# A hybrid decoder layer on one core: five pairs of split weight tiles and four loaded ones instead of four and three

## The chip, the core and the metric

The kernel runs on one core of a Trainium2 chip. A core has five engines with their own instruction queues: TensorE (PE) multiplies matrices, VectorE (DVE), ScalarE (ACT) and GpSimd (POOL) work on elements, SyncE (SP) issues transfers. The metric is the device time of one execution in microseconds; three executions of the kernel before gave 1117.61 to 1118.88 us, median 1118.25 us.

## The reference

One layer of a decoder is computed for 1024 prompt tokens and 8 x 4 sample tokens (T = 1056 tokens of width 1024), in 32-bit floating point:

```
h = rms(x) ;  z = h @ w_in               -> q (512) | k (128) | v (128) | u (512)
a = sliding-window attention(q, k, v)       128 keys, 8 heads, 2 key heads, learned sinks
m = (trailing mean of u, windows 2/4/8/16, minus u) @ w_pool * pool_scale
x = x + rms([a | m] @ w_out)
f = rms(x) ;  f = (silu(f @ w_gate) * (f @ w_up)) @ w_down      width 2816
x = x + rms(f)
x = x + sigmoid(x @ w_ple_gate) * (p @ w_ple)
```

The results are x for both kinds of tokens and the updated key, value and pooling buffers.

## The kernel before

**Products.** Each 32-bit operand is split into a high part in PE's fast format and the low remainder, and a product is made of three: high x high, high x low and low x high (`gemm`, L278). `split` (L163) makes the two parts: ACT casts the high one (L164) and DVE subtracts it to get the low one (L165). The tokens are taken in three groups of 352 columns (g = 0, 1, 2), so almost all matmuls are 128 x 128 by 128 x 352.

**Weights.** Every weight tile of 128 x 1024 numbers (4 KB on each partition) comes through two rings. SP loads it into a raw tile (tag `wr`, W_RAW tiles; `w_load`, L169), and `w_split` (L180) splits it into a pair of tiles (tag `wp`, 2 * W_PAIRS tiles). A ring's tile is given out again when its last user is done: a raw tile when the split has read it, a pair when PE has done its last matmul with it. `weights(j)` (L191) splits up to W_PAIRS - 1 tiles ahead and loads one more; it serves the projections with its default, and the output projections with a count given in the call. `need(k)` (L264) does the same in the FFN and the last stage, four items ahead (LOOK = 4), whatever W_PAIRS is.

```python
def w_load(j):
    ...
    t = wpool.tile(shape, F32, tag="wr", bufs=W_RAW, name=nm("wr"))
    nc.sync.dma_start(t, src)
    ...
def w_tile(shape, s):
    return wpool.tile(shape, F32R, tag="wp", bufs=2 * W_PAIRS, name=nm(s))
    ...
def weights(j, ahead=W_PAIRS - 1):
    for i in range(j, j + (0 if lazy[0] else ahead) + 1):
        w_split(i)
        w_load(i + 1)
```

**Start.** x and the four column tiles of u are loaded in halves in an order pinned on SP (`load`, L342); three of the u tiles use the `wr` ring, the fourth another pool. ACT and DVE make the x operands (L366, L368) and, for the norm, the squares and their sum `acc` (L377, L331 to L334). w_pool (`wpl`, L424) also takes a `wr` tile, then the projections' weights do.

**Attention.** Projections of k, v, q, then blocks of 128 queries, with parts of the output projection as filler between them. The order on PE is that of the program from the u products on.

**FFN.** The hidden width is taken in 11 slabs of two column tiles. Five slabs are first computed for group 2 alone, then six for all three groups, then the first five again for groups 0 and 1 (`WALK`). Groups 0 and 1 are taken together with one product less: POOL makes four sums of the quarters of a gate and an up tile in place (`w_sums`, L990), and ACT and DVE split them into two pairs (`sh`, `sl`). So a column tile takes a pair for gate (jg), one for up (ju) and two for the sums, and a slab two for its part of w_down. The down products of a slab (`down`) run after the gate products of the next slab's first column tile; their results go from PSUM into `o` by DVE (L1087). `hid` is the operand of the down products, made by `hid_put` from `u` (L1068) and `c` (L1061). PE's results stand in eight PSUM banks, each free again when DVE or ACT has read it.

**Last stage.** While groups 0 and 1 go through their last slabs, group 2 is normed (L1115, L1119; `ple_steps`), and then the same happens to groups 0 and 1 beside the final products (`ple_out`).

**The order of the work.** PE's order is pinned. On DVE, ACT, POOL and SP a planner that comes with the language writes the order before the run: it replays the program with its own durations, takes at each engine the earliest instruction of the program that is ready and for which a tile is free, and puts in the waits. Only instructions marked with `keep_in_program_order` keep their place behind the one before. On the chip each queue is worked off strictly in the written order.

Of the kernel before, what the change touches and what calls it, by code (L numbers as in the profile page):

```python
# [47 lines left out]
UEXT = PST + DSEQ  # L48
ULEN = UPRE + SEQ + NDEC * UEXT

W_PAIRS = 4
W_RAW = 3


WARM = 8
# [6 lines left out]
def trunk_kernel(  # L62
# [43 lines left out]
    def nm(s):  # L106
        cnt[0] += 1
        return f"{s}{cnt[0]}"

    def act_tile(shape, dt=F32, s="a"):  # L110
        return apool.tile(shape, dt, tag="a", bufs=A_SLOTS, name=nm(s))
# [57 lines left out]
    def w_load(j):  # L169
        if j >= len(plan) or j in raws:  # L170
            return
        src, shape = plan[j]
        t = wpool.tile(shape, F32, tag="wr", bufs=W_RAW, name=nm("wr"))
        nc.sync.dma_start(t, src)
        raws[j] = t

    def w_tile(shape, s):
        return wpool.tile(shape, F32R, tag="wp", bufs=2 * W_PAIRS, name=nm(s))

# [10 lines left out]
# [5 lines that stand above are left out]
        return pairs[j]  # L195
# [145 lines left out]
    def load(dst, src):  # L341
        tc.keep_in_program_order(nc.sync.dma_start(dst, src))  # L342
# [38 lines left out]
    def u_load(c, h):  # L381
        j = U0[c]
        if h == 0:
            shape = plan[j][1]
            raws[j] = act_tile(shape) if c == 3 else wpool.tile(shape, F32, tag="wr", bufs=W_RAW, name=nm("wr"))
        load(raws[j][:, 4 * h : 4 * h + 4, :], plan[j][0][:, 4 * h : 4 * h + 4, :])
# [34 lines left out]
    for dst, src in ((psc, pscale), (skp, sink_p), (skd, sink_d)):  # L421
        load(dst, src)
    wpl = wpool.tile([P, 4, P], F32, tag="wr", bufs=W_RAW, name="wpl")
    nc.sync.dma_start(wpl, w_pool)  # L424
# [852 lines left out]
```

## Time and profile before

| what | value |
|---|---|
| profiled execution | 1118.37 us, its span 1116.6 us |
| median of three executions | 1118.25 us |
| PE busy | 1106.5 us (99%), 7171 matmuls |
| DVE busy | 748.3 us (67%) |
| ACT busy | 440.0 us (39%) |
| POOL busy | 179.4 us (16%) |
| granted PE clock, mean | 0.998 |
| DMA | 99.54 MB, mean 89 GB/s |

The span is the time from the first to the last instruction. In a list of waits, a row gives who waited, what released it, and the total, the count and the longest in us. In a timeline, a row gives start and length in us, the engine, the line, the operation with out<-in, shapes and count, and in brackets the idle time of the engine before it and what ended it; PEld are the weight loads of PE. In a table of windows, a row gives the window and its length, the busy time of PE, PEld, DVE, ACT and POOL with the number of instructions, PE's granted clock, the DMA share and GB/s. Matmuls overlap: the profile draws each about 0.32 us long although the next starts 0.16 us later.

### The profile page before, as it was taken

How to read it: one execution, taken by the hardware profiler on the slowest of the kernel's cores; microseconds unless marked ns; L12 is line 12 of the kernel's file. 1: busy time of each engine (PE TensorE's matmuls, PEld its weight loads, DVE VectorE, ACT ScalarE, POOL GpSimd, SP SyncE). 2: the span in 40 equal slices, each digit the busy share in tenths (PEclk: the TensorE clock that was granted, in tenths of full speed). 3: DMA queues.
4: the chain of work that ended last, by engine and by line, in shares of the span. 5: the costliest groups of instructions: out<-in, count | busy, mean ns of one | idle time of the engine just before them, and what ended most of it. 6: DMA issues, size and time to landing. Idle time of an engine off the chain costs nothing.

```text
span 1116.6 us, 17703 instructions
## 1 busy us (share of the span) xinstructions
PE 1106.5 (99%) x7171; PEld 1089.6 (98%) x7171; DVE 748.3 (67%) x1241; ACT 440.0 (39%) x779; POOL 179.4 (16%) x152
## 2 busy tenths in 40 slices
PE   8999999999999999999999999999999999999998
PEld 8999988899999999999999999999999999999998
DVE  6667478886979955255564555547887877789532
ACT  8323276664645523331222313123424334365220
POOL 0045032200000131011111102112132123100000
PEclk9999999999999999999999999999999999999999
DMA  8121311542543212121120202122112222336211
GB/s 289 56 71 38 122 43 38 194 157 85 203 166 129 99 38 76 39 76 39 38 60 17 78 36 76 38 100 79 57 58 83 70 76 80 124 133 222 85 58 39
DMA packets 35217, 99.54 MB, mean 89 GB/s; under 512 B 4132, under 2 KB 14660, under 8 KB 35136
## 3 DMA queue, kind: packets, MB, share of 16 engines
q1 hardware_dynamic: 33808, 96.65, 25.5%
q10 hardware_dynamic: 1328, 1.77, 0.5%
q8 instruction: 56, 0.92, 0.3%
q14 instruction: 25, 0.20, 0.1%
HBM read 88.30 MB, written 10.11 MB: 88 GB/s over the span
## 4 chain that ended last, share of the span: by engine, by line
PE 93%; DVE 3%; DMA 1%; issue 1%; POOL 1%; ACT 1%; SPq 0%; DVEq 0%; POOLq 0%
PE b L126 92%; PE b L120 1%; DMA xr<-in_x_dram 1%; DVE wl L165 1%; POOL wr L990 0%; SPq L342 0%; DVE h L368 0%; DVE o L1115 0%; DVE x L1119 0%; DVE mx L628 0%; DVE a L736 0%; DVE p L1024 0%; DVE hid L165 0%; ACT h L366 0%; ACT xr L377 0%
## 5 line engine op out<-in xcount | busy, mean ns | idle before, releaser
L126 PE MATMUL b<-fh,wh 128*128 128x352 f32 x808 | 260.7, 323 | 0.0
L126 PE MATMUL b<-fh,wl 128*128 128x352 f32 x808 | 259.3, 321 | 0.0
L126 PE MATMUL b<-fl,wh 128*128 128x352 f32 x808 | 259.0, 321 | 0.0
L126 PE MATMUL b<-hid,wh 128*128 128x352 f32 x1056 | 252.5, 322 | 1.8 <-DVE o L1115 1.2
L164 ACT CAST wh<-wr 128x1024 fp32r<-128x1024 f32 (+1 forms) x139 | 143.0, 1031 | 248.9 <-PE b L126 205.6
L165 DVE TENSOR_TENSOR wl<-wr,wh 128x1024 fp32r<-128x1024 f32 (+1 forms) x139 | 170.5, 1229 | 57.9 <-ACT wh L164 53.9
L126 PEld LDWEIGHTS b<-hid,wh 128*128 128x128 f32 x1056 | 182.3, 188 | 2.6 <-issue 1.5
L126 PE MATMUL b<-hid,wl 128*128 128x352 f32 x528 | 169.0, 320 | 0.0
L990 POOL TENSOR_TENSOR wr<-wr 128x512 f32<-128x512 f32 x44 | 63.4, 1441 | 623.0 <-DVE wl L165 621.3
L126 PEld LDWEIGHTS b<-fl,wh 128*128 128x128 f32 x808 | 151.9, 188 | 0.0
L126 PEld LDWEIGHTS b<-fh,wl 128*128 128x128 f32 x808 | 151.8, 188 | 0.0
L126 PEld LDWEIGHTS b<-fh,wh 128*128 128x128 f32 x808 | 151.6, 188 | 0.0
L1087 DVE TENSOR_TENSOR o<-o,b 128x352 f32<-128x352 f32 x240 | 114.9, 516 | 29.3 <-PE b L126 29.3
L126 PE MATMUL b<-fh,sh 128*128 128x352 f32 x352 | 113.6, 323 | 0.0
L126 PE MATMUL b<-fl,sh 128*128 128x352 f32 x352 | 112.7, 320 | 0.0
L126 PE MATMUL b<-fh,sl 128*128 128x352 f32 x352 | 112.7, 320 | 0.0
L126 PE MATMUL b<-h,wh 128*128 128x352 f32 x480 | 105.5, 325 | 0.9 <-ACT h L366 0.6
L165 DVE TENSOR_TENSOR sl<-wr,sh 128x1024 fp32r<-128x1024 f32 x44 | 53.8, 1222 | 75.5 <-ACT sh L164 75.5
L126 PEld LDWEIGHTS b<-hid,wl 128*128 128x128 f32 x528 | 98.9, 187 | 0.0
L164 ACT CAST sh<-wr 128x1024 fp32r<-128x1024 f32 x44 | 45.7, 1047 | 130.9 <-POOL wr L990 91.2
L126 PEld LDWEIGHTS b<-h,wh 128*128 128x128 f32 x480 | 81.9, 189 | 2.2 <-DVE h L368 1.2
L126 PE MATMUL b<-h,wl 128*128 128x352 f32 x240 | 66.3, 326 | 0.0
(150 smaller groups left out, 1591.0 us busy)
## 6 DMA issues: line engine op xcount, KB each, us to landing
wr<-in_w_gu_dram SPq DMA_DIRECT2D x64, 512.0 KB, 3.3
wr<-in_w_dn_dram SPq DMA_DIRECT2D x32, 512.0 KB, 3.3
wr<-in_w_pg_dram SPq DMA_DIRECT2D x14, 512.0 KB, 3.6
x<-in_x_dram SPq DMA_DIRECT2D x6, 704.0 KB, 7.1
x1d<-x SPq DMA_DIRECT2D x6, 704.0 KB, 3.5
x<-x1d SPq DMA_DIRECT2D x6, 704.0 KB, 6.7
out_y_dram<-yo SPq DMA_DIRECT2D x24, 176.0 KB, 1.9
wr<-in_w_out_b_dram SPq DMA_DIRECT2D x8, 512.0 KB, 3.3
```

The source lines that it names most:

```text
L120: ins = te.transpose(out, src, ident)
L126: ins = te.matmul(*args, **kw)
L164: fix(se.copy(hi, src))
L165: fix(ve.tensor_tensor(lo, src, hi.bitcast(F32), op=ALU.subtract))
L990: ge.tensor_tensor(out, a, b, op=op)
L1087: ve.tensor_tensor(o, o, v, op=ALU.add)
```

## The change

W_PAIRS goes from 4 to 5 and W_RAW from 3 to 4: ten tiles instead of eight in the ring of split weights, four instead of three in the ring of loaded ones, 12 KB more on each partition. The room comes from the scratch space for descriptors of dynamic DMAs, which the toolkit reserves with 16,384 bytes on each partition and which is set to 1,024. `weights` splits four tiles ahead by default instead of three; the counts given in calls and LOOK stay. The sequence of instructions in the program is otherwise the same.

```diff
-W_PAIRS = 4
-W_RAW = 3
+W_PAIRS = 5
+W_RAW = 4
...
-    nc = _bacc.Bacc("TRN2", target_bir_lowering=False, num_devices=1)
+    nc = _bacc.Bacc("TRN2", target_bir_lowering=False, num_devices=1, dynamic_dma_scratch_size=1024)
```

## The prediction

> **What bounds the kernel now.** I read the page first, then what PE waited for, then PE's share by stage.
>
> ```profile
> span 1116.6 us, 17703 instructions
> ...
> PE 1106.5 (99%) x7171; PEld 1089.6 (98%) x7171; DVE 748.3 (67%) x1241; ACT 440.0 (39%) x779; POOL 179.4 (16%) x152
> ...
> PE b L126 92%; PE b L120 1%; DMA xr<-in_x_dram 1%; DVE wl L165 1%; POOL wr L990 0%; SPq L342 0%; DVE h L368 0%; DVE o L1115 0%; DVE x L1119 0%; DVE mx L628 0%; DVE a L736 0%; DVE p L1024 0%; DVE hid L165 0%; ACT h L366 0%; ACT xr L377 0%
> ```
>
> PE is busy 99% of the span and carries the chain that ended last. A change that leaves the 7171 matmuls alone can only win back PE's waits. These are all that PE had late in the run, and the longest at the start:
>
> ```profile
> PE b L126 <- DVE acc L334: 1.3, 1, 1.3
> PE b L126 <- DVE o L1115: 1.2, 1, 1.2
> ...
> PE b L126 <- DVE hid L165: 0.6, 1, 0.6
> PE b L126 <- DVE dg L312: 0.6, 2, 0.4
> ```
>
> By stage (attention's end and first slabs, the middle slabs, the last five slabs, one undisturbed stretch):
>
> ```profile
> 224.00:395.00 171.00, 171.00 (x1097) 170.87 (x1097) 139.30 (x194) 92.53 (x127) 8.13 (x4) 1.00 0.40 137
> 395.00:800.00 405.00, 405.00 (x2554) 405.00 (x2553) 229.47 (x380) 118.97 (x181) 69.85 (x53) 1.00 0.17 56
> 800.00:1000.00 200.00, 197.86 (x1245) 196.84 (x1243) 159.64 (x254) 79.12 (x110) 44.47 (x32) 1.00 0.27 90
> 868.00:896.00 28.00, 28.00 (x179) 28.00 (x177) 23.84 (x38) 10.81 (x14) 5.49 (x4) 1.00 0.23 76
> ```
>
> PE has no gap between 224 and 800; what there is to win lies in the last slabs and at the start. The undisturbed stretch issues 178 matmuls in 28 us, one per 0.157 us, while each is drawn 0.32 us long. So a stall costs its idle time plus about 0.16 us: 1.2 + 0.16 = 1.38 us for L1115, 0.57 + 0.16 = 0.73 for hid.
>
> **The change part by part.** No instruction is added or removed: the 139 pair splits and 44 sum splits, their loads and matmuls stay. Two kinds of room grow, and with them the order that the planner writes for DVE, ACT and SP can move.
>
> *The scratch space.* I cost it at nothing: every data transfer goes through the two hardware queues.
>
> ```profile
> q1 hardware_dynamic: 33808, 96.65, 25.5%
> q10 hardware_dynamic: 1328, 1.77, 0.5%
> ```
>
> *The fifth pair in the last slabs: the stall before 865.* Here is the chain, from PE's sums (fh,sh), gate (fh,wh) and down products (hid) through ACT, DVE and POOL:
>
> ```profile
> 843.85 0.32 PE L126 MATMUL b<-fh,sh 128*128 128x352 f32 x1
> ...
> 851.48 0.32 PE L126 MATMUL b<-fh,wh 128*128 128x352 f32 x1
> ...
> 855.29 0.48 PE L126 MATMUL b<-hid,wh 128*128 128x352 f32 x2
> ...
> 851.51 1.99 ACT L164 CAST wh<-wr 128x1024 fp32r<-128x1024 f32 x2
> ...
> 854.16 1.22 DVE L165 TENSOR_TENSOR wl<-wr,wh 128x1024 fp32r<-128x1024 f32 x1
> ...
> 855.51 1.45 POOL L990 TENSOR_TENSOR wr<-wr 128x512 f32<-128x512 f32 x1 [16.67 <-DVE wl L165]
> ...
> 859.95 1.28 POOL L990 TENSOR_TENSOR wr<-wr 128x512 f32<-128x512 f32 x1
> ...
> 861.27 1.05 ACT L164 CAST sh<-wr 128x1024 fp32r<-128x1024 f32 x1 [2.90 <-POOL wr L990]
> ...
> 856.37 0.98 DVE L165 TENSOR_TENSOR hid<-u,hid 128x352 fp32r<-128x352 f32 x1 [0.55 <-ACT hid L164]
> ...
> 862.35 1.23 DVE L165 TENSOR_TENSOR sl<-wr,sh 128x1024 fp32r<-128x1024 f32 x1 [3.71 <-ACT sh L164]
> 863.50 1.61 DVE L1115 TENSOR_TENSOR o<-o,b 128x1408 f32<-128x1408 f32 x1
> ```
>
> DVE stands still 3.71 us in front of sl while the down products' banks (o L1087, queued behind it) fill up. Then comes L1115, and only then do banks come free: PE ran dry at 865.25 - 1.38 = 863.9. The sums are late because both casts at 851.51 waited until PE finished the sum products at 851.48; the second feeds POOL. With a fifth pair that second cast needs only the sum pair that is done after 36 of the 48 products, 843.85 + 36 x 0.157 = 849.5. The cast takes 1.05 us and the low half 1.22, done at about 851.9. POOL's four steps take 861.23 - 855.51 = 5.7, to 857.6, the cast 1.05, to 858.7. So sl would end near 859.9 instead of 863.6, L1115 at 861.5, before 863.9: the stall goes, -1.38 us. If the order behind sl changes and the cover of free banks is gone, the 1.38 stays; that is the upper end. I take the whole, since the margin is 2.4 us.
>
> *The same room one slab earlier: the stall before 817.5.*
>
> ```profile
> 809.68 1.22 DVE L165 TENSOR_TENSOR wl<-wr,wh 128x1024 fp32r<-128x1024 f32 x1
> 810.82 1.61 DVE L1115 TENSOR_TENSOR o<-o,b 128x1408 f32<-128x1408 f32 x1
> ...
> 812.79 3.15 DVE L1119 SCALAR_TENSOR_TENSOR x<-o,c,x 128x352 f32<-128x352 f32 x2
> 815.85 1.60 DVE L165 TENSOR_TENSOR hid<-u,hid 128x352 fp32r<-128x352 f32 x1
> ...
> 811.03 1.30 POOL L990 TENSOR_TENSOR wr<-wr 128x512 f32<-128x512 f32 x1 [16.49 <-DVE wl L165]
> ...
> 865.46 1.07 DVE L1119 SCALAR_TENSOR_TENSOR x<-o,c,x 128x352 f32<-128x352 f32 x2
> ```
>
> PE wanted hid at 817.51 - 0.73 = 816.8 and got it at 817.45. One low-half split (1.14 us from start to next start) stands ahead of it that a fifth pair lets go earlier; without it hid ends at 816.3. Term -0.73 us, late next nothing on PE. Bounds: 0 if another split takes its place.
> The rows show something else: L1119 costs 1.6 us each while POOL sums run and 0.53 without, hid 1.60 against the 0.98 above. [...] By the rows alone POOL and DVE move together by that split, so I keep -0.73.
>
> *The fourth loaded tile.* In the slabs SP's loads wait for a free tile, not for bandwidth (busy share 0.27 above):
>
> ```profile
> SPq L174 <- DVE sl L165: 446.2, 44, 28.6
> SPq L174 <- DVE wl L165: 413.8, 81, 22.9
> ```
>
> They come one tile earlier; it is what lets the fifth pair be filled in time, and is worth nothing alone as long as the raw has landed before the pair is free. At the start it changes SP's order:
>
> ```profile
> 13.99 0.34 SPq L424 DMA_DIRECT2D wpl<-in_w_pool_dram  x1
> 14.59 3.22 SPq L174 DMA_DIRECT2D wr<-in_w_in_dram  x2
> 17.86 0.43 SPq L342 DMA_DIRECT2D xr<-in_x_dram  x1
> ```
>
> wpl waits for the first weight's tile now and would not then; one more 512 KB load goes ahead of the last x load at 17.86. The page's bandwidth by slices of 27.9 us starts at 289 GB/s:
>
> ```profile
> GB/s 289 56 71 38 122 43 38 194 157 85 203 166 129 99 38 76 39 76 39 38 60 17 78 36 76 38 100 79 57 58 83 70 76 80 124 133 222 85 58 39
> ```
>
> At that rate 256 KB are 0.9 us and 512 KB 1.8 us. The last x load feeds the third group's products, which follow the 192 of the first two groups, 30 us of PE at 0.157 each, so 1.8 us are covered. wpl costs 0.9 us only if it gets ahead of the x loads that PE waits for; they are pinned in order and stand earlier in the program, so 0, with 0.9 as the other end.
>
> *One split more ahead in the projections (the default of weights()).* ACT and DVE do one split (1.05 and 1.22 us) of w_out before attention instead of in it. None of PE's waits listed above lies there. Term 0; if it delayed an eviction that PE needs, at most those 1.22 us.
>
> *The wait before 1000* is the norm of the PLE input behind a split in DVE's queue:
>
> ```profile
> 997.25 1.22 DVE L165 TENSOR_TENSOR wl<-wr,wh 128x1024 fp32r<-128x1024 f32 x1
> ...
> 1000.03 0.43 PE L126 MATMUL b<-dg,c 88*128 88x352 f32 x1 [0.39 <-DVE dg L312]
> ```
>
> It costs 0.39 + 0.16 = 0.55 us and would go if that split moved forward; it could as well be replaced by the next one. I take 0.
>
> Sum: -1.38 - 0.73 = -2.1 us against the profiled execution's 1118.37 us (span 1116.6 and 1.8 around it, 0.1 above the median of the three): 1116.3 us.
>
> **The rivals.** *A deeper cut:* the split before 1000 moves too (-0.55) and the start's wait of 1.3 + 0.16 us for acc is halved (-0.75): 1115.0. For it: DVE's queue is what PE waits for in all of them. Against: nothing in the change touches acc.
> *No gain:* the planner fills the new room and still puts sl where DVE must wait: 1118.4. DVE's own list speaks for it:
>
> ```profile
> DVE sl L165 <- ACT sh L164: 75.5, 27, 6.1
> ```
>
> It waits for sh in slabs without any stall as well, 27 times, and an order that is off by as much is to be had with five pairs too. Against it: those waits lie where PE has more banks in hand.
>
> *Slower:* sl, ready earlier in the planner's reckoning, is put ahead of the last hid in DVE's queue. There it would wait for POOL until 858.7, end at 859.9, and hid would follow at about 860.9. PE needs that hid after the first group's 24 down products (four tiles of six), 855.29 + 24 x 0.157 = 859.1: 1.8 us of stall in each of five slabs, 9.0 us, less the 2.1 won: 1125.3. It decides as soon as sl stands before hid; two slabs of it cancel the gain, and three make it slower by over 0.2% of the time before if only one stall goes. For it: the gap of 0.55 us before hid at 856.37 is just where a planner that counts POOL as quick would place sl. Against: hid is due sooner once the splits before it are gone.
> *A later start:* wpl ahead of the x loads, 0.9 us, and the longer wait brings a second stretch at the lower clock.
>
> ```profile
> 25.00:30.00 5.00, 4.82 (x22) 4.31 (x20) 4.97 (x12) 4.13 (x8) 0.86 (x2) 0.66 0.02 5
> ```
>
> The granted clock was 0.66 in these five us, a loss of 1.7; a second one makes 2.6 in all, and 1118.9 with the late gains.
>
> **How the numbers follow.** Chances: the forecast 0.38, the deeper cut 0.18, no gain 0.12, sl ahead of hid (in some or all slabs) 0.26, the later start 0.06. A measurement of this kernel tells about 0.2% from no change, 2.2 us: faster is below 1116.0, slower above 1120.5. The forecast's own range is 1115.4 to 1117.4, so some 0.12 of its 0.38 falls below 1116.0. Faster 0.18 + 0.12 = 0.30; slower 0.26; the same 0.44. The range from 1114.8 to 1124.0 leaves out half of the deepest cuts and the slower case's last slabs, 0.2 in all.
>
> **What would show it.** Right: PE's waits for L1115 and for hid are gone from the list, POOL's sums in the last slabs start 3 to 4 us earlier against the first down product, and the share of PE in 800 to 1000 is full. Wrong: a wait of PE for hid of one to two us in several slabs, with sl just ahead of it on DVE; PE waits in the attention stage, where now there are none; a wait of PE for acc above 1.3 us; or unchanged starts of POOL's sums, which would say that the pairs were not what held them.

## The result: half a percent slower

The changed kernel takes 1123.08 us (median of 6 runs, 1122.81 to 1123.63), the kernel before beside it 1117.55 us (6 runs, 1116.94 to 1118.88): ratio 1.0049, 95% interval 1.0036 to 1.0062. That is 5.5 us lost where 2.1 us were to be won. The profiled execution took 1122.84 us.

The page of the changed kernel, its span, engines and chain:

```profile
span 1121.0 us, 17674 instructions
...
PE 1107.4 (99%) x7171; PEld 1090.8 (97%) x7171; DVE 758.5 (68%) x1241; ACT 441.6 (39%) x779; POOL 180.9 (16%) x152
...
PE b L126 76%; POOL wr L990 4%; DMA wr<-in_w_gu_dram 2%; PE b L120 1%; DVE sl L165 1%; DMA xr<-in_x_dram 1%; ACT sh L164 0%; SPq L342 0%; DVE h L368 0%; DVE u L1024 0%; DVE mx L628 0%; DVE a L736 0%; ACT h L366 0%; ACT xr L377 0%; POOL a L642 0%
```

The work is the same: 7171 matmuls and nearly as much time on each engine (DVE 758.5 us after 748.3). In the chain POOL's sums (L990) have grown from 0 to 4%, and their low halves (sl) stand in it with 1%. What PE waited for now, largest first:

```profile
PE b L126 <- DVE c L1024: 3.2, 1, 3.2
PE b L126 <- DVE o L1087: 2.1, 2, 1.7
PE b L126 <- DVE dg L312: 1.3, 2, 0.9
...
PE b L126 <- DVE hid L165: 0.9, 1, 0.9
```

The wait for L1115 is gone, as forecast. In its place stand waits of 3.2 us (L1024), 1.7 and 0.4 us (the two for L1087), and the one for hid has grown from 0.6 to 0.9. By stage:

```profile
224.00:395.00 171.00, 171.00 (x1099) 170.98 (x1098) 142.79 (x194) 93.54 (x129) 9.18 (x4) 1.00 0.39 135
395.00:800.00 405.00, 405.00 (x2553) 405.00 (x2553) 240.29 (x380) 121.42 (x180) 70.74 (x52) 1.00 0.17 57
800.00:1000.00 200.00, 193.82 (x1203) 192.26 (x1202) 151.88 (x242) 73.17 (x105) 43.01 (x32) 0.99 0.27 89
```

From 224 to 800 us PE is as full as before; from 800 to 1000 it issues 1203 matmuls instead of 1245. So the loss lies in the last slabs. The slab with the largest wait, DVE first, then the cast of the up tile and its low half, POOL's first sum, the casts of the sums, and the down products on PE with their first row and the row after the wait:

```profile
856.06 0.98 DVE L165 TENSOR_TENSOR hid<-u,hid 128x352 fp32r<-128x352 f32 x1 [0.55 <-ACT hid L164]
860.67 2.36 DVE L165 TENSOR_TENSOR sl<-wr,sh 128x1024 fp32r<-128x1024 f32 x2 [3.63 <-ACT sh L164]
862.95 0.51 DVE L1024 TENSOR_TENSOR c<-p,b 128x352 f32<-128x352 f32 x1
863.38 0.94 DVE L1087 TENSOR_TENSOR o<-o,b 128x352 f32<-128x352 f32 x2
...
848.81 1.05 ACT L164 CAST wh<-wr 128x1024 fp32r<-128x1024 f32 x1 [0.89 <-ACT wh L164]
...
852.32 1.22 DVE L165 TENSOR_TENSOR wl<-wr,wh 128x1024 fp32r<-128x1024 f32 x1
...
853.61 1.51 POOL L990 TENSOR_TENSOR wr<-wr 128x512 f32<-128x512 f32 x1 [18.05 <-DVE wl L165]
...
859.59 1.99 ACT L164 CAST sh<-wr 128x1024 fp32r<-128x1024 f32 x2 [3.56 <-POOL wr L990]
...
854.44 0.32 PE L126 MATMUL b<-hid,wh 128*128 128x352 f32 x1
...
863.51 0.66 PE L126 MATMUL b<-hid,wh 128*128 128x352 f32 x1 [3.19 <-DVE c L1024]
```

Both low halves of the sums now stand directly behind hid in DVE's queue, ahead of c and of every down result o. DVE waits 3.63 us for POOL and ACT, then works 2.3 us on the two, and reads no bank from 857.0 to 862.95. PE has started the down products at 854.44 and runs out of banks at 863.51 - 3.35 = 860.2 (the 3.19 in brackets and the 0.16 that the prediction adds to each wait). Before, two results were read first, and the second low half came five results later. Its cast had waited for PE, which was still using the pair of tiles that it needed. The kernel before, DVE and then ACT:

```profile
857.71 0.94 DVE L1087 TENSOR_TENSOR o<-o,b 128x352 f32<-128x352 f32 x2
862.35 1.23 DVE L165 TENSOR_TENSOR sl<-wr,sh 128x1024 fp32r<-128x1024 f32 x1 [3.71 <-ACT sh L164]
...
865.03 0.51 DVE L1087 TENSOR_TENSOR o<-o,b 128x352 f32<-128x352 f32 x1
...
866.45 1.81 DVE L1087 TENSOR_TENSOR o<-o,b 128x352 f32<-128x352 f32 x4
868.17 1.22 DVE L165 TENSOR_TENSOR sl<-wr,sh 128x1024 fp32r<-128x1024 f32 x1
...
863.01 1.05 ACT L164 CAST sh<-wr 128x1024 fp32r<-128x1024 f32 x1 [0.69 <-PE b L126]
```

In the changed kernel a stretch at half the clock follows the wait:

```profile
857.00:860.00 3.00, 3.00 (x20) 3.00 (x20) 0.04 (x1) 0.41 (x1) 2.48 (x2) 1.00 0.00 0
860.00:863.40 3.40, 0.33 (x3) 0.04 (x1) 2.73 (x4) 1.58 (x2) 0.00 (x0) 1.00 0.14 31
863.50:866.90 3.40, 3.39 (x12) 3.39 (x13) 3.40 (x6) 0.50 (x1) 0.00 (x0) 0.50 0.78 270
```

In the 3.4 us after it the granted clock is 0.50, and PE issues 12 matmuls, which at 0.159 us each would take 1.9 us: 1.5 us lost. In the window ahead, from 860.0 to 863.4 us, PE worked 0.33 us. Behind the waits of 1.71 us (ended at 910.89) and 0.88 us (at 816.50) the clock stays at 1.00 in the same trace. I take the long wait for the cause; what sets the clock is not shown.

The sum for this pair of traces: late waits of 3.35, 1.87, 0.4 + 0.16 and 0.88 + 0.16 us for L1024, L1087 twice and hid, 6.8 in all, and 1.5 for the clock, against 2.1 before: 6.2 us. The spans differ by 4.4, and the changed kernel's profiled execution was some 1.4 us ahead by the end of attention, so that 5.8 us were lost behind it. The starts differ from trace to trace: of these two, only the kernel before has a stretch at clock 0.50 near 25 us. So I make nothing of that part.

### The profile page after: what moved, and what is told of

Its sections match the earlier page's. It is cut to its first block, busy times and chain, and to the rows that moved or that the text cites. A ratio compares the mean times of both kernels' runs of the same rounds, so it can differ in the third digit from the quotient of the medians.

```text
span 1121.0 us, 17674 instructions
## 1 busy us (share of the span) xinstructions
PE 1107.4 (99%) x7171; PEld 1090.8 (97%) x7171; DVE 758.5 (68%) x1241; ACT 441.6 (39%) x779; POOL 180.9 (16%) x152
## 4 chain that ended last, share of the span: by engine, by line
PE 77%; issue 12%; POOL 5%; DVE 3%; DMA 2%; ACT 1%; SPq 0%; POOLq 0%; DVEq 0%
PE b L126 76%; POOL wr L990 4%; DMA wr<-in_w_gu_dram 2%; PE b L120 1%; DVE sl L165 1%; DMA xr<-in_x_dram 1%; ACT sh L164 0%; SPq L342 0%; DVE h L368 0%; DVE u L1024 0%; DVE mx L628 0%; DVE a L736 0%; ACT h L366 0%; ACT xr L377 0%; POOL a L642 0%
## 5 line engine op out<-in xcount | busy, mean ns | idle before, releaser
L165 DVE TENSOR_TENSOR wl<-wr,wh 128x1024 fp32r<-128x1024 f32 (+1 forms) x139 | 169.8, 1223 | 59.5 <-ACT wh L164 47.1
L990 POOL TENSOR_TENSOR wr<-wr 128x512 f32<-128x512 f32 x44 | 60.0, 1364 | 627.1 <-DVE wl L165 625.3
L1087 DVE TENSOR_TENSOR o<-o,b 128x352 f32<-128x352 f32 x240 | 116.0, 515 | 35.5 <-PE b L126 35.3
L165 DVE TENSOR_TENSOR sl<-wr,sh 128x1024 fp32r<-128x1024 f32 x44 | 53.4, 1222 | 44.2 <-ACT sh L164 44.2
```

Source lines behind the costliest of these rows:

```text
L165: fix(ve.tensor_tensor(lo, src, hi.bitcast(F32), op=ALU.subtract))
L990: ge.tensor_tensor(out, a, b, op=op)
L1087: ve.tensor_tensor(o, o, v, op=ALU.add)
```

## The experiments

All ratios are to the kernel before, run beside each on the same chip. Different experiments ran on different chips, so they are compared by their ratios. An eviction, in the expectations, is the reading of a result out of its PSUM bank.

**The fifth pair alone.** `W_RAW` is back at 3:

```diff
-W_RAW = 4
+W_RAW = 3
```

> The changed kernel with three loaded tiles (W_RAW = 3) and five pairs. Theory A (the fifth pair lets both splits of the four sums stand ahead of the down products' evictions in DVE's queue; PE then runs out of banks): PE's waits of 3.2, 1.7 and 0.4 us before down products in the last slabs stay, 1121 to 1124 us. Theory B (the fourth loaded tile moves SP's loads and with them the order): the waits go, 1116.5 to 1118.5 us.

Measured 1123.57 us, ratio 1.0051 (1.0038 to 1.0064): all of the loss, and the same waits.

```profile
PE b L126 <- DVE c L1024: 2.9, 1, 2.9
PE b L126 <- DVE o L1087: 1.8, 1, 1.8
```

**The fourth loaded tile alone.** `W_PAIRS` is back at 4:

```diff
-W_PAIRS = 5
+W_PAIRS = 4
```

> The changed kernel with four pairs (W_PAIRS = 4) and four loaded tiles. Theory A: the second sum pair still waits for a pair that the down products use, so its low half stays behind several evictions; 1116.5 to 1119 us, PE's late waits like those before (1.2 and 0.6 us). Theory B: 1121 to 1124 us.

Measured 1117.30 us, 0.9996 (0.9987 to 1.0004): no difference. PE's late waits are 0.8 us for L1115 and 0.6 for hid. The first low half again waits behind two results, and the second comes later, by DVE's rows:

```profile
857.90 0.94 DVE L1087 TENSOR_TENSOR o<-o,b 128x352 f32<-128x352 f32 x2
862.58 1.23 DVE L165 TENSOR_TENSOR sl<-wr,sh 128x1024 fp32r<-128x1024 f32 x1 [3.73 <-ACT sh L164]
...
868.40 1.22 DVE L165 TENSOR_TENSOR sl<-wr,sh 128x1024 fp32r<-128x1024 f32 x1
```

Theory B falls; the loss belongs to the ring of pairs.

**The scratch space alone.** The kernel before with it:

```diff
-    nc = _bacc.Bacc("TRN2", target_bir_lowering=False, num_devices=1)
+    nc = _bacc.Bacc("TRN2", target_bir_lowering=False, num_devices=1, dynamic_dma_scratch_size=1024)
```

> The kernel before with the scratch space of 1,024 bytes and nothing else. Theory A: no transfer uses it and all tiles only move to other addresses: 1117 to 1118.5 us, no measurable difference. If addresses or descriptors mattered: 1120 us or more.

Measured 1117.45 us, 0.9992 (0.9984 to 1.0001): no difference.

**Three splits ahead in the projections.** The changed kernel with the old default:

```diff
-    def weights(j, ahead=W_PAIRS - 1):
+    def weights(j, ahead=3):
```

> The changed kernel with three splits ahead in the projections, as before, instead of four. Theory A: the loss lies in the last slabs, 1122 to 1124 us. If the earlier splits in the projections cost anything: 1 us or more below the changed kernel.

Measured 1124.26 us, 1.0059 (1.0047 to 1.0071). No cost of the early splits shows; the loss stays.

**Order alone.** The changed kernel, its two low halves tied behind the fourth down result in the slabs of the three waits for banks. Rings, loads and splits stay as changed; `los` holds the two low halves.

```diff
+            ins = ve.tensor_tensor(o, o, v, op=ALU.add)
+            evicted[0] += 1
+            if AHEAD + 6 < n < END and evicted[0] == 4:
+                for lo in los:
+                    tc.add_manual_dep(lo.ins, ins.ins.name, ...)
```

> The changed kernel with nothing moved but the place of the sums' two low halves in DVE's queue: in the slabs of the three stalls they stand behind the fourth eviction of the down products. Theory A: DVE waits for POOL later, with four banks already free, and the three waits (with the stretch at half clock some 6 us) shrink to under 1.5 us in all: 1116.5 to 1119 us. If the order on DVE is not the cause: 1122 to 1124 us, as changed.

Measured 1117.61 us, 0.9990 (0.9981 to 0.9999): the whole loss is won back by an order. DVE's rows in the slab shown above:

```profile
857.51 0.94 DVE L1091 TENSOR_TENSOR o<-o,b 128x352 f32<-128x352 f32 x2
858.37 1.61 DVE L1128 TENSOR_TENSOR o<-o,b 128x1408 f32<-128x1408 f32 x1
859.90 0.51 DVE L1091 TENSOR_TENSOR o<-o,b 128x352 f32<-128x352 f32 x1
860.34 1.07 DVE L1132 SCALAR_TENSOR_TENSOR x<-o,c,x 128x352 f32<-128x352 f32 x2
861.33 0.51 DVE L1091 TENSOR_TENSOR o<-o,b 128x352 f32<-128x352 f32 x1
861.76 2.35 DVE L998 TENSOR_TENSOR sl<-wr,sh 128x1024 fp32r<-128x1024 f32 x2
```

What stood still for 3.63 us now reads banks, and when DVE comes to sl the sums are there: no wait in brackets. (L1091, L1128, L1132 and L998 are L1087, L1115, L1119 and the sums' L165 of the other kernels.) Elsewhere DVE works in the same order in both traces, but for one swap of neighbours near 886 us. That the order written for DVE is the cause is shown; why the planner chose it (by durations that make POOL look quick, as the prediction supposed) is not.

**The second low half alone** behind the fourth result, the first left ahead of all:

```diff
-                for lo in los:
+                for lo in los[1:]:
```

> The changed kernel with only the second low half of the sums held behind the fourth eviction, the first left where it is, ahead of all evictions. DVE stops for POOL as early and as long as in the changed kernel, but comes to the evictions 1.14 us sooner. If the length of the stop is what counts: the waits of 3.2, 1.7 and 0.4 us become some 2.1, 0.5 and 0: 1119 to 1121 us. If it is the second low half that does the harm: 1117 to 1118 us, as with both held.

Measured 1121.44 us, 1.0032 (1.0020 to 1.0044), with the waits

```profile
PE b L126 <- DVE c L1028: 2.1, 1, 2.1
...
PE b L126 <- DVE o L1091: 1.0, 1, 1.0
```

Where both ahead cost 3.2 and 1.7 us, one costs 2.1 and 1.0: the length of DVE's stop counts, and the first low half has the larger share of it. The time lies above the forecast of 1119 to 1121. The second wait stayed longer than forecast, and there is a new one of 0.9 us for hid near 901 us, which I have not explained.

**The order in the first of the last slabs too.** There the changed kernel has a low half ahead of hid itself:

```profile
814.79 1.23 DVE L165 TENSOR_TENSOR sl<-wr,sh 128x1024 fp32r<-128x1024 f32 x1 [0.30 <-ACT sh L164]
815.93 0.52 DVE L165 TENSOR_TENSOR hid<-u,hid 128x352 fp32r<-128x352 f32 x1
```

```diff
-            if AHEAD + 6 < n < END and evicted[0] == 4:
+            if AHEAD + 6 <= n < END and evicted[0] == 4:
```

> As the run with the low halves behind the fourth eviction, and so in the first of the last slabs too, where the changed kernel's DVE has a low half of the sums ahead of hid and PE waits 0.9 us for hid. Theory A: that wait of 0.9 + 0.16 us goes as well: 1 us under the run before it, 1116 to 1117.5 us. If hid is late for the PLE input's L1119 alone: no difference, 1117 to 1118.

> The quickest kernel so far a second time (five pairs, four loaded, low halves behind the fourth eviction). Theory C: its trace again shows no wait of PE between 800 and 1000 us and a pace of 158.9 ns there; 1114 to 1116 us. If its first trace was luck: a slower pace there without a wait.

Measured 1114.75 us, 0.9980 (0.9971 to 0.9988), and the second time 1114.62 us, 0.9964 (0.9951 to 0.9978). It has the lowest median here, 2.8 to 3.8 us under the kernel before and below the forecast of 1116 to 1117.5. hid comes earlier now, with the sums behind four results: PE's wait for it shrinks from 0.9 to 0.1 us, and between 800 and 1000 us neither trace has another but 0.4 us for dg near the end. DVE's rows:

```profile
815.26 0.53 DVE L165 TENSOR_TENSOR hid<-u,hid 128x352 fp32r<-128x352 f32 x1 [0.69 <-ACT hid L164]
815.71 1.81 DVE L1091 TENSOR_TENSOR o<-o,b 128x352 f32<-128x352 f32 x4
817.43 2.35 DVE L998 TENSOR_TENSOR sl<-wr,sh 128x1024 fp32r<-128x1024 f32 x2
```

By the ratios the gain over the run before it is 1.1 us the first time (0.9980 after 0.9990), about what the wait of 1.06 is worth, and 2.9 the second (0.9964). The kept traces differ by some 3 us in span; the last section says where the rest of that lies.

**The same order with three loaded tiles** (`W_RAW = 3` in that kernel):

> Five pairs and three loaded tiles with the low halves behind the fourth eviction in all the slabs concerned. If the fifth pair alone makes the rest of the gain: as with four loaded tiles, 1114 to 1116 us. If the fourth loaded tile is needed for it: 1116.5 us or more.

Measured 1116.04 us, 0.9971 (0.9960 to 0.9982), in two groups, 1114.4 to 1114.9 and 1116.0 to 1116.4. The fourth loaded tile is not needed for most of the gain; whether it adds the rest these runs can't tell.

**The kernel before with its low halves behind the sixth result**, first without and then with the first of the last slabs:

> The kernel before (four pairs, three loaded) with the low halves of the sums behind the sixth eviction in the last slabs but the first. Theory A: DVE serves six banks before it waits for POOL, so the wait of 1.2 + 0.16 us for L1115 goes: 1116 to 1117.3 us. If L1115 itself holds the banks: no difference, 1117.5 to 1118.5 us.

> The kernel before (four pairs, three loaded) with the sums' low halves behind the sixth eviction in all of the last slabs where PE waits, the first included. Theory A (PE's waits alone): both waits, 1.36 and 0.73 us, go, 1115.5 to 1116.5 us. Theory C (after each wait PE restarts in one of three paces, 158.9, 160.0 or 161.1 ns per matmul, and keeps it to the next wait): a kernel without late waits keeps the quick pace through the last slabs, so its times also lie closer together: 1115 to 1116.5 us, within 1.5 us of each other in most runs.

Measured 1118.05 us, 1.0001 (0.9992 to 1.0009), and 1115.80 us, 0.9975 (0.9966 to 0.9985). In both traces the wait for L1115 is gone and the one for hid stays at 0.6 us; the second was forecast to go and didn't. So one missing wait of 1.38 us makes 2.6 us in one kernel and nothing in the other, whose runs lie between 1115.1 and 1120.0 although its trace has the same late waits as the other's; that trace is of its quickest run. This spread speaks against theory C, and I leave it unexplained. But with four pairs and three loaded tiles, too, an order made the kernel 2.6 us quicker (0.9975), about as much as with the larger rings (0.9980 and 0.9964).

**The sums' low halves on POOL**, in the changed kernel:

```diff
-            split(*hl, src)
+            se.copy(hl[0], src)
+            ge.tensor_tensor(hl[1], src, hl[0].bitcast(F32), op=ALU.subtract)
```

> The changed kernel (five pairs, four loaded) with the low halves of the sums made by POOL instead of DVE: 44 subtractions of 1.2 us leave DVE's queue, POOL's sums take some 5 us longer. Theory A: DVE no longer waits for the sums, so PE's waits of 3.2, 1.7 and 0.4 us go: 1115.5 to 1118 us. Theory B, or a POOL that is too slow: 1121 us or more, with PE waiting for the sums themselves.

Measured 1119.19 us, 1.0014 (1.0005 to 1.0023). The time lies between the two forecasts. The three waits for banks go, as by theory A, but in the slab where group 2 is normed PE waits 0.8 and then 2.0 us for hid, and from 820.0 to 823.4 us the granted clock is 0.50 (0.94 over the 30 us from 820 to 850, in which PE issues 179 matmuls, after 191 in the changed kernel). DVE's rows and POOL's:

```profile
810.99 2.78 DVE L1120 SCALAR_TENSOR_TENSOR x<-o,c,x 128x352 f32<-128x352 f32 x2
813.70 1.60 DVE L1069 TENSOR_TENSOR u<-u,p 128x352 f32<-128x352 f32 x1
...
816.41 2.39 DVE L165 TENSOR_TENSOR hid<-u,hid 128x352 fp32r<-128x352 f32 x1 [0.69 <-ACT hid L164]
...
816.07 4.97 POOL L995 TENSOR_TENSOR sl<-wr,sh 128x1024 fp32r<-128x1024 f32 x2 [1.16 <-ACT sh L994]
```

hid takes 2.39 us, from 816.41 to 818.80, inside the 4.97 us in which POOL makes the two low halves; in the quickest kernel it took 0.53 (815.26 above). That POOL's work held it up is my reading of these rows; how it would do so they do not show. Work taken off DVE came back as a longer instruction of DVE's own, and PE waited for it.

## Why the prediction was wrong

*What bounds the kernel* was right: PE's waits in the last slabs decided, and between 224 and 800 us PE has no gap in either trace. The spacing of 0.157 us was read from a window's count, which takes in two matmuls begun before it; between starts it is 0.159, too little to matter.

*The scratch space* at nothing, *the fourth loaded tile* worth nothing alone, and *one split more ahead* at nothing: right by the three runs (0.9992, 0.9996, and 1.0059 without it). Nor was the fourth loaded tile needed to fill the fifth pair: with three the loss was the same (1.0051). One detail was wrong: wpl did get ahead of an x load at the start (8.38 us against 10.30), but the run with four loaded tiles alone has that order too (8.63 and 10.70) and lost nothing. The later start did not come.

*The fifth pair in the last slabs, -1.38 us*, is the step that failed, in two places. It let POOL start at 851.9, taking the cast and its low half to be done by then. The cast came when forecast: 848.81 is 5.6 us before the first down product at 854.44, and the forecast 849.5 is 5.8 before the one at 855.29. But its low half stood behind DVE's gate and up results and ran at 852.32, so POOL started at 853.61, 0.8 us before the first down product instead of 3.4. And the step followed only the first low half, and left the results between the two where they were. Before, the second sum pair had to wait for a pair that the down products were using, and that lack of room kept the second low half behind seven results; with four pairs it came late again, with five it did not. The fifth pair removed the lack, and the planner put both low halves ahead of all results. The prediction's upper end for this term, "the 1.38 stays", had no such case: where it forecast 1.38 us won, PE's waits in three slabs were 3.35 + 1.87 + 0.56, and the clock cost 1.5 more.

*The stall before 817.5, -0.73 us*: hid did not come earlier, it came later, at 0.88 + 0.16 us. One split did go ahead of it, but a low half of the sums took its place; the rival "sl ahead of hid" is what happened in this one slab, and the run with the order kept in it too brought that wait down to 0.1 us.

*The slower rival* named the right queue and the right instruction, but in three slabs of four the wrong victim: not hid, but the results behind it. Its reason, a planner that takes POOL for quick, fits, but no run tests it. Its 1.8 us a slab were 3.35, 1.87 and 0.56. It had 0.26. *No gain* gave the reason why the change could not keep its promise (DVE waits for sh wherever sl stands), but took it for harmless. The range up to 1124.0 takes in 1123.1 only because it was drawn to hold part of this rival; the forecast itself, 1116.3, was off by 6.8 us and in the wrong direction.

*The wait before 1000*, taken as unchanged, is: 0.4 of the 1.3 us that stand above for dg. Its other 0.9 us lie at the start, where dg has taken the place of acc, the wait that the deeper cut hoped to halve.

## What to carry to other kernels

A larger ring is not only room: where a queue is written ahead by a planner, a lack of tiles can be what holds a slow producer's consumer back, and more room lets it stand in front of work that frees another ring, here the PSUM banks. When more tiles are added, follow every instruction that the old ring held back, not only the first, and look what is queued behind it and how long the banks last (here six down products of 0.95 us each, from 854.44 to 860.2). The room cost 5.5 us with the order that the planner wrote. With the order of two instructions on DVE written by hand the kernel was about 3 us quicker than before, but so it was, within the noise, with one of the two orders in the old rings (0.9975): that the room itself is worth anything is not shown.

## What I had not expected

PE's pace in undisturbed stretches is not one number. The mean spacing of the 128 x 128 by 128 x 352 matmuls, taken from their starts in ten-microsecond pieces, is 158.9, 160.0 or 161.1 ns, constant for many pieces, at a granted clock of 1.00. From 816 us on, where it changes, PE has waited just there; near 801 us it goes from 161.1 to 158.9 in every trace, there without a wait. The windows from 870 to 980 us of the kernel before, of the order in three slabs, and of the quickest kernel, none of which has a wait inside:

```profile
870.00:980.00 110.00, 110.00 (x694) 110.00 (x693) 84.90 (x134) 41.98 (x56) 27.61 (x20) 1.00 0.28 95
```

```profile
870.00:980.00 110.00, 110.00 (x685) 110.00 (x684) 80.36 (x127) 40.72 (x56) 26.74 (x20) 1.00 0.28 92
```

```profile
870.00:980.00 110.00, 110.00 (x694) 110.00 (x694) 81.28 (x127) 40.54 (x57) 26.69 (x20) 1.00 0.30 101
```

685 matmuls instead of 694 are 9 x 0.159 = 1.4 us in these 110 us. It may be why the order in three slabs has runs at 1115.5 as well as at 1118.3. The five traces without a wait of over 0.6 us between 800 and 1000 us (the quickest kernel twice, the one with three loaded tiles, and the two orders of four pairs) all issue 1009 matmuls from 820 to 980 us; the order in three slabs, with 0.9 us before 820 and no wait behind it, issues 995. That is 14 x 0.159 = 2.2 us, and with the wait for hid it makes up the 3 us between these traces. Three of the five are of executions among the quickest of their kernel, so how the slower ones run is not known. A wait is followed now by one pace, now by another: after the same 0.6 us for hid it was 158.9 ns in the kernel before and 161.1 with the scratch space alone. So a wait of PE may cost more than its length; what sets the pace I did not find out.
